# Four heads of values per matmul, and sums of squares from high and low parts, in a transformer block

## The chip, the cores and the metric

The kernel runs on one core of a Trainium2 chip. The metric is the device time of one launch in microseconds (us). Engines are named as in the profile: PE is TensorE (PEld its weight loads), DVE is VectorE, ACT is ScalarE, POOL is GpSimd, and SP is the engine from whose queue all of this kernel's DMAs are issued.

## What is computed

One layer of a hybrid encoder on 1024 tokens with 1024 channels, in float32. Cut to what matters:

```python
u = modulate(rmsnorm(h, g_ff1), sh1, sc1)
h = h + 0.5 * gt1 * swiglu(u, w1_gate, w1_up, w1_down)      # D_FF = 2816
u = modulate(rmsnorm(h, g_mix), sh2, sc2)
proj = u @ w_in
qa, ka, va, xm, o_pre, ga, gb = split(proj)                  # each 1024 wide
ya = diff_attention(rope(qa), rope(ka), va)                  # 8 heads, values 128 wide; rmsnorm per head
yb = mlstm_branch(xm, o_pre)                                 # 4 heads, chunkwise
merged = sigmoid(ga) * (ya @ w_proj_a) + sigmoid(gb) * (yb @ w_proj_b)
h = h + gt2 * (merged @ w_out)
u = modulate(rmsnorm(h, g_ff2), sh3, sc3)
h = h + 0.5 * gt3 * swiglu(u, w2_gate, w2_up, w2_down)
return rmsnorm(h, g_final)
```

Each rmsnorm needs a sum of squares over channels for every token. sh, sc and gt come from the conditioning vector c through w_ada ("ada").

## The kernel before

**Layout.** Channels lie on the 128 partitions, tokens along the free dimension, in two halves of 512. A float32 product is made of three float32r matmuls: an operand is split into a high part (an ACT cast, L126, L137, L143) and a low part (a DVE subtraction, L127, L138, L144), and `mm3` (L132 to L134) adds high x high, high x low and low x high in PSUM. `unit` (L121) loads a weight tile of 128 x 1024 (raw, two buffers in `wraw`) and splits it into a pair wh, wl from the pool `whl`, which has three buffers of each. `t512` hands out one of six shared tiles of 128 x 512.

**Stages, in order.** The first feed-forward block (to some 690 us); the projections in for the mLSTM branch with its convolution and its output gate (`stage_in`, to some 895 us; its first group of three weight units is run half by half in `first_norm` and `group`); `stage_mlstm` (to some 1205 us); `stage_attn` (to some 1800 us); the rest of the gated branch, and `stage_merge` (to some 2027 us); the second feed-forward block with the final norm (`out_tail`, `out_step`).

**Order of the work.** PE runs its instructions in the order in which the program emits them. The other engines and the DMA queue of SP also run in order, but their order is made by a planner (the tile framework) from priorities and its own estimate of durations. In the mLSTM and attention stages `paced` emits the steps of the mixers by due times in a model of PE time, and between them pieces of dense work from a list of jobs: `job_qk` (rotary queries and keys of a head), `job_v` (values), `job_g` (pre-activations of the branch gates), `job_b` (gated mLSTM branch). The string `order` sets their sequence: one job of queries and keys, four of values, then queries, keys and gates. A job yields after six matmuls and says what they cost in the model. In the mLSTM stage the scores of a block are due at t and its values at t + 6, and a pitch is 3.

**Values.** `job_v(hp)` projects the values of two heads: for each of 8 token tiles, 8 channel tiles x 3 matmuls (L899 to L901) with the token tile as weights and 256 columns of w_v moving. Its two weight units stay in place for the whole job. ACT copies the result (L906) into a tile vo of its own, and every second token tile a DMA of 256 KB stores it to `vd` in DRAM. `load_v` in the attention stage reads a head from there.

**Sums of squares.** ACT squares (L208, L605, L1338), DVE adds channel tiles together (L210, L611), and PE sums over partitions with one float32 matmul on a 128 x 128 tile of ones: in `rstd` (L182, at the start of the kernel), `rstd_half` (L215), `out_stat` (L629) and, per head, `norm_items` (L1345, into a PSUM tile oss that shares its one bank with the attention's output po). `rstd_of` (L157) makes the reciprocal root on ACT (L162, L165), in a t512 tile.

Of the kernel before, what the change touches and what calls it, by code (L numbers as in the profile page):

```python
# [20 lines left out]
P = 128  # L21
D = 1024
# [17 lines left out]
class Halves:  # L40
    """two tiles with half of the tokens each"""
# [9 lines left out]
class Net:  # L51
    def __init__(self, ctx, tc, aps, dbg):
# [5 lines left out]
        self.whl = e(tc.tile_pool(name="whl", bufs=3))  # L58
# [7 lines left out]
        nc.vector.memset(self.ones, 1.0)  # L66
        self.zeros = c.tile([P, 64], F32, name="zeros")
# [24 lines left out]
    # conditioning: one column block of w_ada per call  # L92
# [27 lines left out]
    # weights  # L120
# [19 lines left out]
    def split_in(self, hi, lo):  # L140
        """the same of what has been loaded into the place of the low part"""
        raw = lo.bitcast(F32)
        self.nc.scalar.copy(hi, raw)  # L143
        self.nc.vector.tensor_sub(lo, raw, hi.bitcast(F32))  # L144

    def set_lnexp(self, after):
        """have the table set with Ln and Exp loaded behind `after`"""
        t = self.nc.scalar.preload_act_table_set(LNEXP)
        self.after(t, after)
        return t  # L150
# [6 lines left out]
    def rstd_of(self, ps, n, last):  # L157
        """1 / sqrt(ps / n + eps); `last`: the activation before it"""
# [9 lines left out]
    # 1 / rms over channels, on every partition, for some of the tokens  # L168
# [35 lines left out]
    def sum_square(self, n, i, m):  # L204
        """add channel tile m of half n, its i-th, to the running sum of squares"""
# [6 lines left out]

    def rstd_half(self, bank):
        ps = bank()
        self.nc.tensor.matmul(ps, self.ones, self.sq_acc, start=True, stop=True)  # L215
        self.r_half = self.rstd_of(ps, D, self.sq_last)
# [7 lines left out]
    def norm_step(self, i, q, j, bank):  # L224
        """first half's modulation behind the steps of the last products"""
# [8 lines left out]
    def norm_behind(self, i, n, m, bank):  # L234
        """behind the update of channel tile m of half n: statistics, and the first half's modulation"""
# [12 lines left out]
    def group(self, srcs, psp, tag, hook):  # L248
        """several M-tiles of a projection of u at once, channel tile by channel tile"""
# [15 lines left out]
    def ffn(self, wgu, wd, gt, first, plain, hid, after, step, extra=None):  # L265
        """h += gate * (silu(u w_gate) * (u w_up)) w_down; hidden passes through DRAM"""
# [33 lines left out]
    # The hidden layer goes to DRAM as the operands that down() takes: even tiles are its rows b1., odd ones b2.  # L300
# [9 lines left out]
    def store_right(self, hid, f, c2):  # L310
        """what follows from the second token half of tile f"""
# [8 lines left out]
    def store_left(self, hid, f, c1):  # L320
        """what follows from the first token half, behind store_right"""
# [10 lines left out]
    # One level of Strassen's scheme in Winograd's form: 7 products for the 8 of two tiles of w^T u, with  # L332
    # w^T = [a11 a12; a21 a22] (tiles x channel halves) and u = [b11 b12; b21 b22] (channel x token halves)
# [10 lines left out]
    def combine_u(self, x, pool):  # L344
        """t1 = b12 - b11, t2 = b22 - t1, -t4 = b21 - t2 for one channel tile of each half"""
# [20 lines left out]
    def combine_u3(self, x):  # L366
        """t3 = b22 - b12, in the place of b12"""
# [69 lines left out]
    def down(self, wd, gt, hid, psg, tp, after, step):  # L437
        """the same scheme for w_down^T (channel halves x even and odd tiles) and the hidden layer"""
# [63 lines left out]
        # product: its operands, weights to fetch meanwhile, a combination that takes a weight's place  # L502
# [43 lines left out]
    def first_start(self, srcs, psg, gtag, psd, dtag):  # L546
        """the first block's input: statistics, modulation and the first tiles as x and w_ada come in"""
# [42 lines left out]
    def first_norm(self, i, srcs, psg, gtag, psd, dtag):  # L590
        """later blocks' input: the first tiles run on one half while the other is normalised"""
# [8 lines left out]
    def out_tail(self, n, i, m, bank):  # L600
        """final norm behind the last update of h"""
# [23 lines left out]
    def out_stat(self, q, sums, bank):  # L625
        ns = self.spans[q]
        ps = bank()[:, 0:ns.stop - ns.start]
        for i, x in enumerate(sums):
            self.nc.tensor.matmul(ps, self.ones, x, start=i == 0, stop=i == len(sums) - 1)  # L629
# [8 lines left out]
    # one M-tile of a projection of u: PSUM halves  # L638
# [18 lines left out]
    def mix_setup(self):  # L657
# [11 lines left out]
        self.vd = [sc(f"v{h}", [P, 2, 8, P]) for h in range(4)]  # L669
# [4 lines left out]
    def fold_gates(self, hd, psp, tag):  # L674
        """gate weights seen from xc and xm, as [hi | lo] stationary tiles"""
# [32 lines left out]
    def stage_in(self, st):  # L708
        """xm with causal conv and gate pre-activations; sigmoid of the output gate"""
# [178 lines left out]
    # dense work that fills the tensor engine between the steps of the two sequence mixers  # L888
    def job_v(self, hp):
        nc = self.nc  # L890
        w = [self.unit(self.a["wv"][hp, i]) for i in range(2)]
        for tt in range(8):
            ps = self.psdn.tile([P, NW], F32, name=self.nm("vp"), tag="dn")
            tsl = slice(tt * P, tt * P + P)
            o = ps[:, 0:256]
            for k in range(KT):
                wh, wl = w[k // 4]
                ws = slice((k % 4) * 256, (k % 4) * 256 + 256)
                nc.tensor.matmul(o, self.uh[k][:, tsl], wh[:, ws], start=k == 0, stop=False)  # L899
                nc.tensor.matmul(o, self.uh[k][:, tsl], wl[:, ws], start=False, stop=False)  # L900
                nc.tensor.matmul(o, self.ul[k][:, tsl], wh[:, ws], start=False, stop=k == KT - 1)  # L901
                if k % 2:
                    if k == KT - 1:
                        if tt % 2 == 0:
                            vo = self.rope.tile([P, 2, 2, P], F32, name=self.nm("vo"), tag=f"vo{tt // 2 % 2}")
                        nc.scalar.copy(vo[:, :, tt % 2], o.rearrange("p (q c) -> p q c", q=2))  # L906
                        if tt % 2:
                            nc.sync.dma_start(out=self.vd[hp][:, :, tt - 1:tt + 1], in_=vo)
                    yield 6 * 0.11
# [672 lines left out]
```

## Time and profile before

| | |
|---|---|
| median of three timed runs | 2677.02 us (2673.28 to 2679.34) |
| profiled execution, span from the first to the last instruction | 2681.1 us |
| PE busy | 2592.6 us (97%) in 12704 matmuls |
| DVE busy | 1877.3 us (70%) |
| ACT busy | 1288.3 us (48%) |
| mean granted clock of PE | 0.990 |

The page gives no other time of the profiled execution than its span. Matmuls are pipelined: the duration of one in the trace is its latency, and the next one starts before it ends. The granted clock has two levels here, 1.0 (2.4 GHz) and 0.5 (1.2 GHz).

### The profile page before, as it was taken

How to read it: one execution, taken by the hardware profiler on the slowest of the kernel's cores; microseconds unless marked ns; L12 is line 12 of the kernel's file. 1: busy time of each engine (PE TensorE's matmuls, PEld its weight loads, DVE VectorE, ACT ScalarE, POOL GpSimd, SP SyncE). 2: the span in 40 equal slices, each digit the busy share in tenths (PEclk: the TensorE clock that was granted, in tenths of full speed). 3: DMA queues.
4: the chain of work that ended last, by engine and by line, in shares of the span. 5: the costliest groups of instructions: out<-in, count | busy, mean ns of one | idle time of the engine just before them, and what ended most of it. 6: DMA issues, size and time to landing. Idle time of an engine off the chain costs nothing.

```text
span 2681.1 us, 35203 instructions
## 1 busy us (share of the span) xinstructions
PE 2592.6 (97%) x12704; PEld 2155.8 (80%) x12704; DVE 1877.3 (70%) x3352; ACT 1288.3 (48%) x2369; POOL 22.5 (1%) x85
## 2 busy tenths in 40 slices
PE   6999999999899999999999999999999999999998
PEld 4888887778777799997777778777887888888886
DVE  7987878678795456646766766654467776766867
ACT  6333333446435366654666766753345332323444
POOL 0000000000000000000000000000000000000000
PEclk8999999999999999999999999999999999999999
DMA  7434345833674423334333333558342333236533
GB/s 262 162 130 145 118 149 185 274 99 104 215 258 149 140 91 118 111 100 121 111 102 106 99 105 115 159 198 277 131 140 87 110 98 115 99 102 216 161 95 122
DMA packets 174471, 380.47 MB, mean 142 GB/s; under 512 B 18405, under 2 KB 47529, under 8 KB 174297
## 3 DMA queue, kind: packets, MB, share of 16 engines
q1 hardware_dynamic: 174296, 378.24, 43.6%
q8 instruction: 99, 1.62, 0.2%
q14 instruction: 76, 0.61, 0.1%
HBM read 280.27 MB, written 97.90 MB: 141 GB/s over the span
## 4 chain that ended last, share of the span: by engine, by line
PE 84%; DMA 7%; DVE 5%; ACT 3%; issue 1%; SPq 0%; DVEq 0%; ACTq 0%; POOL 0%; POOLq 0%
PE gu L134 10%; PE gu L133 10%; PE gu L132 10%; PE acc L132 5%; PE acc L133 5%; PE acc L134 5%; PE ab L132 2%; PE ab L133 2%; PE ab L134 2%; PE dn L134 2%; PE dn L132 2%; PE dn L133 2%; PE gp L132 2%; PE gp L134 2%; PE gp L133 2%; PE pt L1305 1%
## 5 line engine op out<-in xcount | busy, mean ns | idle before, releaser
L132 PE MATMUL gu<-uh,wh 128*128 128x512 f32 x800 | 314.2, 393 | 10.1 <-ACT uh L201 8.8
L133 PE MATMUL gu<-ul,wh 128*128 128x512 f32 x800 | 313.4, 392 | 1.3 <-DVE ul L202 1.3
L134 PE MATMUL gu<-uh,wl 128*128 128x512 f32 x800 | 313.2, 391 | 0.8 <-DVE wl L127 0.7
L137 ACT CAST wh<-wr 128x512 fp32r<-128x512 f32 x228 | 134.0, 619 | 253.0 <-PE gu L133 194.0
L132 PE MATMUL acc<-uh,wh 128*128 128x512 f32 x616 | 241.9, 393 | 1.3 <-ACT uh L137 1.3
L133 PE MATMUL acc<-ul,wh 128*128 128x512 f32 x616 | 240.3, 390 | 1.3 <-DVE ul L138 1.3
L134 PE MATMUL acc<-uh,wl 128*128 128x512 f32 x616 | 239.8, 389 | 0.0
L126 ACT CAST wh<-wr 128x1024 fp32r<-128x1024 f32 x120 | 125.8, 1049 | 148.0 <-PE wo L133 46.1
L127 DVE TENSOR_TENSOR wl<-wr,wh 128x1024 fp32r<-128x1024 f32 x120 | 146.5, 1221 | 71.8 <-ACT wh L126 70.9
L132 PEld LDWEIGHTS gu<-uh,wh 128*128 128x128 f32 x800 | 151.2, 189 | 44.3 <-ACT uh L201 10.4
L133 PEld LDWEIGHTS gu<-ul,wh 128*128 128x128 f32 x800 | 151.2, 189 | 34.4 <-DVE ul L202 2.3
L134 PEld LDWEIGHTS gu<-uh,wl 128*128 128x128 f32 x800 | 151.1, 189 | 33.4 <-DVE wl L127 2.3
L133 PE MATMUL gu<-ut,wh 128*128 128x512 f32 x456 | 177.5, 389 | 0.0
L132 PE MATMUL gu<-ut,wh 128*128 128x512 f32 x456 | 177.4, 389 | 0.0
L134 PE MATMUL gu<-ut,wl 128*128 128x512 f32 x456 | 177.4, 389 | 0.0
L138 DVE TENSOR_TENSOR wl<-wr,wh 128x512 fp32r<-128x512 f32 x228 | 152.8, 685 | 1.6 <-ACT wh L137 1.6
L137 ACT CAST uh<-hr 128x512 fp32r<-128x512 f32 x154 | 95.4, 619 | 100.2 <-PE acc L134 63.6
L132 PEld LDWEIGHTS acc<-uh,wh 128*128 128x128 f32 x616 | 115.6, 188 | 28.6 <-ACT uh L137 2.5
L133 PEld LDWEIGHTS acc<-ul,wh 128*128 128x128 f32 x616 | 115.6, 188 | 26.3 <-DVE ul L138 2.2
L134 PEld LDWEIGHTS acc<-uh,wl 128*128 128x128 f32 x616 | 115.6, 188 | 24.1
L138 DVE TENSOR_TENSOR ul<-hr,uh 128x512 fp32r<-128x512 f32 x154 | 105.8, 687 | 35.5 <-ACT uh L137 35.0
L1281 ACT ACTIVATE p<-sc,lr 128x256 f32<-128x256 f32 (+7 forms) x128 | 94.8, 741 | 74.0 <-DVE lr L1279 72.1
(335 smaller groups left out, 6561.4 us busy)
## 6 DMA issues: line engine op xcount, KB each, us to landing
ada<-wada SPq DMA_DIRECT2D x72, 512.0 KB
wr<-win SPq DMA_DIRECT2D x48, 512.0 KB
wr<-w1gu SPq DMA_DIRECT2D x44, 512.0 KB
wr<-w2gu SPq DMA_DIRECT2D x44, 512.0 KB
wr<-wab SPq DMA_DIRECT2D x32, 512.0 KB
g<-t SPq DMA_DIRECT2D x32, 256.0 KB
t<-g SPq DMA_DIRECT2D x32, 256.0 KB
wr<-wout SPq DMA_DIRECT2D x16, 512.0 KB
```

Source lines behind the costliest of these rows:

```text
L126: nc.scalar.copy(hi, raw)
L127: nc.vector.tensor_sub(lo, raw, hi.bitcast(F32))
L132: nc.tensor.matmul(ps, w[0], x[0], start=start, stop=False)
L133: nc.tensor.matmul(ps, w[0], x[1], start=False, stop=False)
L134: nc.tensor.matmul(ps, w[1], x[0], start=False, stop=stop)
L137: (eng or self.nc.scalar).copy(hi, src)
L138: self.nc.vector.tensor_sub(lo, src, hi.bitcast(F32))
L1281: nc.scalar.activation(pc[c][:, 0:W], ps[:, 0:W], AF.Exp, bias=lr[:, 2 + c:3 + c], accum_out=lr[:, c:c + 1])
L1305: nc.tensor.transpose(pt[:, kk, i], a[i][:, kb * P:kb * P + P], self.ident)
```

## The change

Values are projected for four heads in a job: four weight units, 512 columns per matmul, two jobs and not four. The result is copied into a shared t512 tile and stored for each token tile. `sum_over` takes the place of the float32 matmul on ones in `rstd_half`, `out_stat` and `norm_items`: it splits its operand into a high and a low part, in two t512 tiles, and runs two float32r matmuls on a float32r tile of ones. `rstd` keeps the float32 matmul. The pool `whl` gets five buffers, and the DMA scratch of the program is set to 1024. Comments go as well.

```diff
-        self.whl = e(tc.tile_pool(name="whl", bufs=3))
+        self.whl = e(tc.tile_pool(name="whl", bufs=5))
...
+        self.onesr = c.tile([P, P], F32R, name="onesr")
+        nc.scalar.copy(self.onesr, self.ones)
...
+    def sum_over(self, ps, x, start=True, stop=True):
+
+        hi, lo = (self.t512()[:, 0:x.shape[1]].bitcast(F32R) for _ in range(2))
+        self.split(x, hi, lo)
+        self.nc.tensor.matmul(ps, self.onesr, hi, start=start, stop=False)
+        self.nc.tensor.matmul(ps, self.onesr, lo, start=False, stop=stop)
+
     def rstd_half(self, bank):
         ps = bank()
-        self.nc.tensor.matmul(ps, self.ones, self.sq_acc, start=True, stop=True)
+        self.sum_over(ps, self.sq_acc)
...
         for i, x in enumerate(sums):
-            self.nc.tensor.matmul(ps, self.ones, x, start=i == 0, stop=i == len(sums) - 1)
+            self.sum_over(ps, x, i == 0, i == len(sums) - 1)
...
-        self.vd = [sc(f"v{h}", [P, 2, 8, P]) for h in range(4)]
+        self.vd = [sc(f"v{h}", [P, 4, 8, P]) for h in range(2)]
...
     def job_v(self, hp):
-        nc = self.nc
-        w = [self.unit(self.a["wv"][hp, i]) for i in range(2)]
+
+        nc = self.nc
+        w = [self.unit(self.a["wv"][hp, i]) for i in range(4)]
         for tt in range(8):
             ps = self.psdn.tile([P, NW], F32, name=self.nm("vp"), tag="dn")
             tsl = slice(tt * P, tt * P + P)
-            o = ps[:, 0:256]
             for k in range(KT):
-                wh, wl = w[k // 4]
-                ws = slice((k % 4) * 256, (k % 4) * 256 + 256)
-                nc.tensor.matmul(o, self.uh[k][:, tsl], wh[:, ws], start=k == 0, stop=False)
-                nc.tensor.matmul(o, self.uh[k][:, tsl], wl[:, ws], start=False, stop=False)
-                nc.tensor.matmul(o, self.ul[k][:, tsl], wh[:, ws], start=False, stop=k == KT - 1)
+                wh, wl = w[k // 2]
+                ws = slice((k % 2) * NW, (k % 2) * NW + NW)
+                nc.tensor.matmul(ps, self.uh[k][:, tsl], wh[:, ws], start=k == 0, stop=False)
+                nc.tensor.matmul(ps, self.uh[k][:, tsl], wl[:, ws], start=False, stop=False)
+                nc.tensor.matmul(ps, self.ul[k][:, tsl], wh[:, ws], start=False, stop=k == KT - 1)
                 if k % 2:
                     if k == KT - 1:
-                        if tt % 2 == 0:
-                            vo = self.rope.tile([P, 2, 2, P], F32, name=self.nm("vo"), tag=f"vo{tt // 2 % 2}")
-                        nc.scalar.copy(vo[:, :, tt % 2], o.rearrange("p (q c) -> p q c", q=2))
-                        if tt % 2:
-                            nc.sync.dma_start(out=self.vd[hp][:, :, tt - 1:tt + 1], in_=vo)
-                    yield 6 * 0.11
+                        vo = self.t512().rearrange("p (q c) -> p q c", q=4)
+                        nc.scalar.copy(vo, ps.rearrange("p (q c) -> p q c", q=4))
+                        nc.sync.dma_start(out=self.vd[hp][:, :, tt], in_=vo)
+                    yield 6 * 0.216
...
-                nc.sync.dma_start(out=v[1].bitcast(F32), in_=self.vd[hd // 2][:, hd % 2])
+                nc.sync.dma_start(out=v[1].bitcast(F32), in_=self.vd[hd // 4][:, hd % 4])
...
-                    nc.tensor.matmul(ps, self.ones, sqs[n], start=True, stop=True)
+                    self.sum_over(ps, sqs[n])
...
-            order = "qvvvvqqqggqggqggqggqgggggggg"
-            src = {"q": [net.job_qk(hd) for hd in range(8)], "v": [net.job_v(hp) for hp in range(4)],
+            order = "qvvqqqggqggqggqggqgggggggg"
+            src = {"q": [net.job_qk(hd) for hd in range(8)], "v": [net.job_v(hp) for hp in range(2)],
...
-    o["wv"] = win[:, 2048:3072].reshape(2, 4, P, 4, 256).transpose(3, 0, 2, 1, 4).reshape(4, 2, P, D)
+    o["wv"] = win[:, 2048:3072].reshape(4, 2, P, 2, NW).transpose(3, 0, 2, 1, 4).reshape(2, 4, P, D)
...
-    nc = _bacc.Bacc("TRN2", target_bir_lowering=False, num_devices=1)
+    nc = _bacc.Bacc("TRN2", target_bir_lowering=False, num_devices=1, dynamic_dma_scratch_size=1024)
```

## Rows read from the trace of the kernel before

**Rows 1.** The head of the page: the span, and PE's busy time.

```profile
span 2681.1 us, 35203 instructions
PE 2592.6 (97%) x12704; PEld 2155.8 (80%) x12704; DVE 1877.3 (70%) x3352; ACT 1288.3 (48%) x2369; POOL 22.5 (1%) x85
```

**Rows 2.** By stretch, us: length, busy PE, PEld, DVE, ACT, POOL, clock, DMA share, GB/s.

```profile
60.00:660.00 600.00, 597.86 (x2634) 486.40 (x2633) 479.56 (x814) 228.75 (x391) 0.00 (x0) 1.00 0.46 150
...
720.00:920.00 200.00, 189.89 (x846) 150.14 (x845) 127.99 (x238) 83.62 (x111) 0.62 (x6) 0.98 0.56 190
920.00:1210.00 290.00, 284.11 (x2260) 274.22 (x2259) 170.37 (x446) 177.12 (x523) 13.94 (x32) 1.00 0.34 108
1210.00:1800.00 590.00, 562.97 (x2835) 464.51 (x2834) 397.85 (x746) 381.92 (x690) 6.49 (x32) 0.99 0.40 120
```

**Rows 3.** PE's groups by line and shape: busy us, mean ns, idle before, releasers.

```profile
L132 PE MATMUL gu<-uh,wh 128*128 128x512 f32 x800 | 314.2, 393 | 10.1 <-ACT uh L201 8.8 <-ACT wh L126 1.3
...
L134 PE MATMUL dn<-uh,wl 128*128 128x512 f32 x256 | 101.1, 395 | 6.5 <-DVE wl L127 6.5
...
L899 PE MATMUL vp<-wh,uh 128*128 128x256 f32 x256 | 73.7, 288 | 0.0
```

**Rows 4.** PE in order of time, value matmuls: start, us, what; twelve from first to last.

```profile
935.08 0.28 PE L899 MATMUL vp<-wh,uh 128*128 128x256 f32 x1
...
936.51 0.28 PE L1135 MATMUL num<-mv,sch 128*128 128x258 f32 x1
```

**Rows 5.** PE in order of time, twelve query matmuls from first to last row.

```profile
927.57 0.39 PE L132 MATMUL qp<-uh,wh 128*128 128x512 f32 x1
...
930.32 0.28 PE L1108 MATMUL pr<-RHL,selr 128*128 128x256 f32 x1
```

**Rows 6.** All engines in order of time, around a sum of squares of the second norm.

```profile
695.66 0.68 DVE L210 TENSOR_TENSOR t<-t,t 128x512 f32<-128x512 f32 x1
...
702.00 1.02 PE L215 MATMUL nps<-t,ones 128*128 128x512 f32 x2
...
703.09 0.40 PE L133 MATMUL dn<-ul,wh 128*128 128x512 f32 x1
```

**Rows 7.** The page's costliest groups: a split of 128 x 512, cast and subtraction.

```profile
L137 ACT CAST uh<-hr 128x512 fp32r<-128x512 f32 x154 | 95.4, 619 | 100.2 <-PE acc L134 63.6
...
L138 DVE TENSOR_TENSOR ul<-hr,uh 128x512 fp32r<-128x512 f32 x154 | 105.8, 687 | 35.5 <-ACT uh L137 35.0
```

**Rows 8.** ACT, DVE and PE in order of time, projections in; idle before in brackets.

```profile
728.03 1.06 ACT L126 CAST wh<-wr 128x1024 fp32r<-128x1024 f32 x1 [8.12 <-PE dn L133]
...
728.35 1.23 DVE L115 SCALAR_TENSOR_TENSOR ada<-ada,crep 128x1024 f32<-128x1024 f32 x1 [2.56 <-DMA ada<-wada]
...
735.41 0.80 PE L134 MATMUL dn<-uh,wl 128*128 128x512 f32 x1 [5.37 <-DVE wl L127]
```

**Rows 9.** Busy time by stretch, as rows 2, behind that wait.

```profile
735.40:740.20 4.80, 4.79 (x11) 3.80 (x12) 4.80 (x5) 0.00 (x0) 0.00 (x0) 0.50 0.96 311
740.20:745.00 4.80, 4.80 (x22) 3.92 (x21) 4.80 (x6) 2.30 (x2) 0.11 (x1) 1.00 0.29 117
```

**Rows 10.** ACT and PE in order of time, a head's norm in attention.

```profile
1378.87 0.69 ACT L162 ACTIVATE t<-oss,epsc 128x512 f32<-128x512 f32 x1 [3.60 <-DMA qk<-t]
...
1379.61 1.12 PE L1345 MATMUL oss<-t,ones 128*128 128x512 f32 x2 [1.81 <-ACT t L162]
```

**Rows 11.** ACT and PE in order of time, the next head's norm.

```profile
1440.65 0.63 ACT L1338 ACTIVATE t<-osb 128x512 f32<-128x512 f32 x1
...
1444.86 1.02 PE L1345 MATMUL oss<-t,ones 128*128 128x512 f32 x2
```

**Rows 12.** All engines in order of time, the last norm of the kernel.

```profile
2668.79 0.63 ACT L605 ACTIVATE t<-h 128x512 f32<-128x512 f32 x1 [1.42 <-DVE h L474]
2669.47 1.13 PE L629 MATMUL acc<-t,ones 128*128 128x512 f32 x2 [0.20 <-ACT t L605]
2670.63 0.69 ACT L162 ACTIVATE t<-acc,epsc 128x512 f32<-128x512 f32 x1 [1.22 <-PE acc L629]
```

## The prediction, made before the change was run

> **What bounds the kernel now.** I read first the head of the page: TensorE (PE) has work in flight for 2592.6 of 2681.1 us [rows 1], so time goes only if PE work or a PE wait goes. The busy time by stage, second, shows where waits are left: in the feed-forward stretch PE is busy 597.9 of 600 us; behind it that falls to 189.9 of 200 (projections in), 284.1 of 290 (mLSTM) and 563.0 of 590 (attention), where VectorE (DVE) and ScalarE (ACT) are busy two thirds of the time [rows 2]. Third, a matmul's listed duration (283 to 288 ns for a value matmul [rows 3]) is its latency, and matmuls overlap; what one costs is the spacing of starts, read from the order in time. Fourth, I looked up what PE waited for where it stood still, to see which of those waits hang on something that the change touches: weight halves (wh, wl) and the six shared 512-wide tiles (t512).
>
> The span is 4.1 us above the median of the three timed runs (2677.0); I sum changes against the span and take them off the median.
>
> **Values, four heads at once.** Removed: 768 matmuls of 256 columns (three lines of 256 [rows 3]); added: 384 of 512. Twelve value matmuls start within 936.51 - 935.08 = 1.43 us, 0.119 us each [rows 4]. Twelve query matmuls of 512 columns in the same stage take 930.32 - 927.57 = 2.75 us, 0.229 us each [rows 5]. 768 x 0.119 = 91.4 us, 384 x 0.229 = 87.9: 3.5 us less on a PE that has no wait in these lines [rows 3]. The time goes only if PE then doesn't wait for the mLSTM steps that run between these pieces: a piece of the filling work is now six matmuls of 512 columns (1.37 us) and not of 256 (0.71). The steps are placed two pitches apart from what they wait for, which is more than one piece, so I take -3.5, with 0 and -5 as ends.
>
> The Trainium skill, "TensorE: Matmul & The Clock Gate", section "Back-to-back issue gap", gives a spacing of N / 2.4 + 2.5 ns for N columns at the full clock, which puts nearly the whole cost on the columns. By it (an estimate) 768 x 109.2 ns = 83.9 us would become 384 x 215.8 ns = 82.9 us, and this part would bring 1.0 us, not 3.5. The rows above, 119 and 229 ns, don't follow it at 256 columns, and I go by them.
>
> The rest of this part costs nothing on the path. The evacuations go from 32 copies of 256 columns to 16 of 512. The stores stay 16 of 256 KB on SP, in runs half as long; behind each stand the loads of the mLSTM heads, as before, and the first reader of a value is the attention stage. The weights stay eight loads of 512 KB. Four weight units must now be held at once; with five pairs one is spare, as with two of three before, and the hand-over from the first job to the second happens once, not three times. There the last two units need a raw buffer and a freed pair in turn; I allow up to 3 us of PE wait in the range and 0 in the sum, since the fourth is needed only three pieces into the job, with mLSTM steps between.
>
> **Sums of squares.** Removed: a float32 matmul on the tile of ones, which the trace records as two. From the start of one to the start of the second matmul behind it are 703.09 - 702.00 = 1.09 us [rows 6]; less one ordinary matmul (0.23) it costs 0.86 us. Added: two matmuls of 512 columns, 0.46 us, so 0.40 less on PE each; and ahead of them an ACT cast (0.62 us) and a DVE subtraction (0.69 us) [rows 7], 1.31 us in series. There are 23: 16 in attention (8 heads, two halves), four between the feed-forward, mixing and merge stages, three for the output. The sums at the start of the kernel stay float32.
> Of the four and the first output sum, the running sum is finished well before its place in PE's order: the one in rows 6 at 695.66 + 0.68 = 696.34, 5.7 us ahead, which holds the split. 5 x 0.40 = -2.0 us.
> The last two stand at the end with nothing beside them. The last Square ends at 2668.79 + 0.63 = 2669.42; the matmul begins at 2669.47 and the logarithm at 2670.63 [rows 12], 1.2 us later. Afterwards a cast, a subtraction and one matmul's latency (0.39 [rows 3]) lie there: 0.62 + 0.69 + 0.39, with hops of 0.05, 1.85 us. +0.6.
> Attention: 16 x 0.40 = -6.4 us of PE. Against that, (i) the split must fit between the Square and the matmul. In the usual case it does: Square ends at 1440.65 + 0.63 = 1441.28, the matmul starts at 1444.86, a gap of 3.6 us [rows 11]; one of the sixteen had no gap, where 1.3 us show. (ii) The sum now takes two of the six t512 tiles, and these are scarce here: once ACT waited 3.60 us for a DMA out of a t512 tile before it could write the reciprocal root, and PE stood 1.81 us at the next sum [rows 10]. Two more of these are 3.6 us. (iii) ACT gets 16 x 0.62 = 9.9 and DVE 16 x 0.69 = 11.0 us more, on 382 and 398 of 590 [rows 2]. Behind them on DVE stand the splits that PE's transposes wait for; that is in (ii)'s allowance. +5 in all, net -1.4. Ends: -6.4 (all hidden) and 16 x (1.31 - 0.40) = +14.6 (all shown).
>
> **Five pairs of split weights, not three.** The diff's first lines raise whl from 3 to 5 and pay with the smaller DMA scratch and the dropped vo tiles. At the start of the projections in, three units are held by the first group until its end. So ACT's cast of the fourth waits 8.12 us until 728.03; behind it DVE, in order, first does ada columns that wait for their loads (2.56 us before one of them); the low half comes so late that PE stands 5.37 us until 735.41 [rows 8]. With five pairs the fourth unit can be split as soon as its load is in, while the first group still runs, and PE has nothing to wait for there: -5.4. The granted clock is 0.50 behind this stall, over 4.8 us with 11 matmuls where the next 4.8 us have 22 [rows 9]; without the stall I expect none of that, -2.4. All other PE waits for wh or wl in the trace are 6.5 - 5.4 = 1.1 (dn) and 1.3 (gu) [rows 3], and fall where a group takes three pairs from the stage before: half of 2.4, -1.2. The feed-forward stretches have nothing to gain, as PE is full there [rows 2]. Together -9.0, ends 0 and -10.5.
>
> **Sum.** -3.5 - 2.0 + 0.6 - 1.4 - 9.0 = -15.3 us: a profile of 2665.8, and 2677.0 - 15.3 = 2661.7 us.
>
> **Rivals.**
> (A) The forecast, 2661.7.
> (B) All splits in attention ride free (-5.0 more) and deeper weights take away some of its own waits, 27 us of PE idle [rows 2], say a fifth (5): -25, 2651.7. For it: casts of weights in attention wait for PE to free a pair, in an in-order queue ahead of the mixers' casts. Against: PE's named waits in that stage are for the attention's own splits.
> (C) The change of depth doesn't do what I say: DVE keeps the ada columns ahead of the low half, and the stall of 5.4 and the slow clock stay. -15.3 + 7.8 = -7.5, 2669.5. For it: that order isn't written in the kernel but comes from a planner. Against: the wait that began it is the freed pair, 8.12 us.
> (D) Half of the attention's splits show: 8 x 1.31 - 6.4 = +4.1, not -1.4, and the hand-over between the value jobs costs 3 us: -15.3 + 5.5 + 3 = -6.8, 2670.2.
> (E) Slower: t512 runs out in attention. A head's turn has two Squares, four halves and two roots, eight tiles for six places, beside the rotary work and the gates, whose tiles wait for DMAs out. If ACT, in order, stands 3.6 us for a place [rows 10] and PE with it, and the clock then drops as in rows 9 (2.4 us), one event costs 6 us. It decides from (15.3 + 5.4) / 6 = 3.5 events on; five give 30 - 15.3 = +15, 2692. For it: rows 10 show the wait. Against: once in 16 so far, and halves are given back as soon as PE has read them.
>
> **How the numbers follow.** A 0.50, B 0.15, C 0.12, D 0.12, E 0.11. About 0.2% (5.4 us) is what a measurement of this kernel can tell from no change: faster means below 2671.6. A and B lie there wholly, C and D by a bit, with half of each over the line when the other terms come out smaller: 0.50 + 0.15 + 0.06 + 0.06 = 0.77. The other halves are within: 0.12. E is slower: 0.11. The range of A alone is about 2654 to 2669; to leave out no more than 2 in 10 it takes in B's centre, C and D and the near edge of E: 2644 to 2679.
>
> **What would show it.** Value matmuls of 512 columns 384 times at 0.229 us, and the mLSTM stretch 3 to 4 us shorter. Sums as pairs of matmuls of 0.23 us; the cast and subtraction between Square and sum in 3 us. No PE wait near 730, no 0.50 clock behind it, and the projections in 8 us shorter. The attention stretch within 5 us of before; a PE wait on the cast of a sum, or ACT on a DMA out of a t512 tile, more than three times there would mean D or E. What would make it wrong: a planner's new order of ACT, DVE and SP that makes a stall elsewhere, above all where the stages meet.

## The result, and the profile after

The changed kernel takes 2703.03 us (median of four runs, 2699.05 to 2706.9), the kernel before 2678.18 (four runs): a ratio of 1.0097, interval 1.0085 to 1.0109, 25 us slower by the medians. I had put 2661.7 first, and a range up to 2679.

Head of the page of the changed kernel, then its busy time by stretch (us: length, busy PE, PEld, DVE, ACT, POOL, clock, DMA share, GB/s), answering [rows 1] and [rows 2]:

```profile
span 2703.0 us, 34689 instructions
...
PE 2591.9 (96%) x12320; PEld 2142.6 (79%) x12320; DVE 1893.9 (70%) x3375; ACT 1301.5 (48%) x2378; POOL 21.8 (1%) x85
```

```profile
60.00:660.00 600.00, 596.42 (x2627) 485.31 (x2627) 480.45 (x815) 228.32 (x392) 0.00 (x0) 1.00 0.46 150
720.00:920.00 200.00, 193.70 (x871) 154.02 (x870) 130.74 (x242) 86.18 (x116) 0.62 (x6) 0.99 0.57 191
920.00:1210.00 290.00, 282.43 (x1872) 254.90 (x1871) 166.13 (x443) 173.65 (x500) 13.29 (x32) 1.00 0.34 104
1210.00:1800.00 590.00, 541.41 (x2714) 447.98 (x2714) 401.27 (x750) 379.58 (x688) 6.51 (x32) 0.97 0.38 113
```

In the projections in, PE is busier by 3.8 us (193.70 against 189.89). In attention it is busy for 21.6 us less of 590 (541.41 against 562.97), with 121 fewer matmuls done, and the mean clock has gone from 0.99 to 0.97, worth 0.02 x 590 = 12 us of full clock. The loss is in attention.

I also measure stages by marks on PE that all kernels share: first matmul of the projections in, first query matmul, first score of attention, last matmul on its output po. Before, these stages take 201.5, 327.5 and 555.2 us; after, 193.7, 330.0 and 583.0. So projections in -7.8, mLSTM +2.5, attention +27.8; what comes behind it is 3.6 us shorter, and the first block 2.9 longer. Together +21.8, the difference of the two spans.

What PE waited for in the changed kernel (us in total, times, longest), the rows for the sums and the one left for the projections in, where no row for a weight half stands any more:

```profile
PE oss L219 <- ACT t L139: 19.3, 9, 6.2
...
PE oss L220 <- DVE t L140: 7.5, 12, 1.7
...
PE dn L134 <- DVE h L483: 2.5, 1, 2.5
```

The sums of attention wait 19.3 us for the cast (L139) and 7.5 for the subtraction (L140): 26.8 us in 21 waits. Before, one wait of 1.8 us [rows 10] and one of 0.6 stood there. The longest, ACT and then PE in order of time (start, duration; idle before in brackets), with the busy time of the stretch behind:

```profile
1446.19 0.63 ACT L1345 ACTIVATE t<-osb 128x512 f32<-128x512 f32 x1
1446.72 0.60 ACT L139 CAST t<-t 128x512 fp32r<-128x512 f32 x1
...
1453.13 1.04 ACT L145 CAST av<-av 128x1024 fp32r<-128x1024 f32 x1 [3.52 <-DMA av<-v]
1454.08 0.62 ACT L167 ACTIVATE t<-t 128x512 f32<-128x512 f32 x1
1454.62 0.57 ACT L944 COPY t<-qp 128x512 f32<-128x512 f32 x1
1455.08 1.04 ACT L128 CAST wh<-wr 128x1024 fp32r<-128x1024 f32 x1
...
1457.41 0.61 ACT L139 CAST t<-t 128x512 fp32r<-128x512 f32 x1
```

```profile
1447.38 0.50 PE L219 MATMUL oss<-t,onesr 128*128 128x512 f32 x1 [1.28 <-ACT t L139]
...
1458.07 0.79 PE L219 MATMUL oss<-t,onesr 128*128 128x512 f32 x1 [6.20 <-ACT t L139]
1459.76 0.80 PE L220 MATMUL oss<-t,onesr 128*128 128x512 f32 x1 [0.90 <-DVE t L140]
```

```profile
1454.40:1464.40 10.00, 5.43 (x12) 3.97 (x13) 8.14 (x13) 4.33 (x8) 0.00 (x0) 0.50 0.32 96
1464.40:1474.40 10.00, 10.00 (x53) 8.47 (x53) 5.40 (x12) 6.00 (x12) 0.20 (x1) 1.00 0.25 93
```

The Square of the second half (L1345) ends at 1446.82. Its cast starts at 1457.41, 10.6 us later, behind a load of values on which ACT stands 3.52 us, a root, a copy, the cast of a weight and an exponential. Note the first cast shown, of the first half: it too stands only behind the second half's Square, 3.9 us after its own. Over the sixteen sums of attention the cast starts 0.8 to 36 us behind the end of its Square, 4.6 at the median; PE waits where the matmul is due earlier than that.

Before, the matmul read the Square itself, so ACT had nothing more to do for it [rows 11]. ACT stood as long for a load of values there too, but the sum's matmul, at 1444.86, did not depend on what stood behind. ACT in the trace of before:

```profile
1447.82 1.05 ACT L143 CAST av<-av 128x1024 fp32r<-128x1024 f32 x1 [3.71 <-DMA av<-v]
```

The first of the two stretches of 10 us above begins 3.7 us before the wait ends; PE's granted clock is 0.50 in it, and it has 12 matmuls where the next has 53. In all, attention has eight stretches at 0.50 in the trace of after, 38 us together, and five of them (27 us) begin in or right behind waits of a sum; before, it had three, 14 us.

The values do what they were to do: 384 matmuls of 512 columns, six of them here within one piece, 0.23 us apart, as [rows 5].

```profile
931.90 0.40 PE L908 MATMUL vp<-wh,uh 128*128 128x512 f32 x1
...
933.05 0.39 PE L910 MATMUL vp<-wh,ul 128*128 128x512 f32 x1
934.81 0.39 PE L908 MATMUL vp<-wh,uh 128*128 128x512 f32 x1
```

### The profile page after: what moved, and what is told of

Its sections match the earlier page's. It is cut to its first block, busy times and chain, and to the rows that moved or that the text cites. A ratio compares the mean times of both kernels' runs of the same rounds, so it can differ in the third digit from the quotient of the medians.

```text
span 2703.0 us, 34689 instructions
## 1 busy us (share of the span) xinstructions
PE 2591.9 (96%) x12320; PEld 2142.6 (79%) x12320; DVE 1893.9 (70%) x3375; ACT 1301.5 (48%) x2378; POOL 21.8 (1%) x85
## 4 chain that ended last, share of the span: by engine, by line
PE 56%; DMA 5%; DVE 5%; ACT 3%; issue 1%; SPq 0%; DVEq 0%; ACTq 0%
PE gu L136 5%; PE gu L134 5%; PE gu L135 5%; PE acc L134 3%; PE acc L136 3%; PE acc L135 3%; PE ab L134 2%; PE ab L135 2%; PE ab L136 2%; PE gp L134 2%; PE gp L135 2%; PE gp L136 2%; PE wo L135 1%; PE wo L134 1%; PE wo L136 1%
## 5 line engine op out<-in xcount | busy, mean ns | idle before, releaser
L139 ACT CAST wh<-wr 128x512 fp32r<-128x512 f32 x228 | 133.8, 620 | 220.9 <-PE gu L135 194.9
L139 ACT CAST uh<-hr 128x512 fp32r<-128x512 f32 x154 | 95.1, 619 | 133.4 <-PE acc L136 54.8
L140 DVE TENSOR_TENSOR wl<-wr,wh 128x512 fp32r<-128x512 f32 x228 | 152.6, 686 | 2.5 <-ACT wh L139 2.4
L140 DVE TENSOR_TENSOR ul<-hr,uh 128x512 fp32r<-128x512 f32 x154 | 105.6, 687 | 36.8 <-ACT uh L139 36.7
```

Of the source, the lines that this page charges most:

```text
L139: (eng or self.nc.scalar).copy(hi, src)
L140: self.nc.vector.tensor_sub(lo, src, hi.bitcast(F32))
```

## The experiments

Times are medians, each against the runs of the kernel before on the same chip (2677.8 to 2680.3 in the batches below). The ratio weighs all runs, and by it a difference comes out up to some 2 us other than by the medians; both are given where that matters. Single executions of one kernel differ by up to some 10 us either way, so stage lengths of single traces are read with that in mind.

**The sums of attention taken back.** The changed kernel with L1352 as before:

```diff
-                    self.sum_over(ps, sqs[n])
+                    nc.tensor.matmul(ps, self.ones, sqs[n], start=True, stop=True)
```

> The changed kernel with one part undone: the sums of the attention's norms go back to the float32 matmul. Theory Q (the cast and the subtraction of these sums stand in ACT's and DVE's queues and PE waits for them, 19.3 + 7.5 us of waits plus slow clock): the attention stretch falls back by 25 to 30 us, the whole to 2673 to 2680 us. Rival T (the stretch is longer for another reason: the values now take t512 tiles, or five pairs of weights reorder the queues): no more than 10 us come back, 2693 us or more.

Measured: 2678.15, ratio 0.9991 (0.9978 to 1.0004), 25 us faster than the changed kernel. Attention takes 555.8 us. The whole loss goes with these 16 sums.

**The sums of attention alone.** The kernel before, three pairs and narrow values, with the 16 sums split as in the change, in t512 tiles.

```diff
-                    nc.tensor.matmul(ps, self.ones, sqs[n], start=True, stop=True)
+                    hi, lo = (self.t512().bitcast(F32R) for _ in range(2))
+                    self.split(sqs[n], hi, lo)
+                    nc.tensor.matmul(ps, self.onesr, hi, start=True, stop=False)
+                    nc.tensor.matmul(ps, self.onesr, lo, start=False, stop=True)
```

> The kernel before with the attention's sums alone as two passes in t512 tiles, three pairs of weights, values as before. Theory: the splits wait for places in t512 and in ACT's queue whatever the rest does, so 15 to 30 us more than before: 2692 to 2707 us. Rival: it takes the deeper weights or the values' use of t512 to make it slow: within 8 us of before.

Measured: 2705.92, ratio 1.0111 (1.0097 to 1.0126), 28 us slower than before. Attention takes 584.4 us. What PE waited for, as above:

```profile
PE oss L1349 <- ACT t L139: 26.0, 11, 6.7
...
PE oss L1350 <- DVE t L140: 7.3, 11, 3.0
```

So neither the wide values nor the five pairs are needed for the loss. In the longest of these waits the shared tiles show directly: the cast of the sum at 1379.76 has 4.71 us of idle ACT before it, ended by a DMA out of a t512 tile (`qk<-t`), and PE waits 6.69 us for that cast.

**Tiles of their own.** The changed kernel; the halves of a sum of attention go into two own tiles and not into t512, at the same place in the program.

```diff
-                    self.sum_over(ps, sqs[n])
+                    hi, lo = (a1.tile([P, NW], F32R, name=self.nm("so"), tag=f"so{c}", bufs=1) for c in "hl")
+                    self.split(sqs[n], hi, lo)
+                    nc.tensor.matmul(ps, self.onesr, hi, start=True, stop=False)
+                    nc.tensor.matmul(ps, self.onesr, lo, start=False, stop=True)
```

> The changed kernel with a high and a low tile of their own for the attention's sums in place of two t512 tiles. If places in t512 are what delays the cast (my prediction's rival E), 15 us or more come back: 2688 us or less. If it is the place of the cast in ACT's queue, behind loads of values, copies and weight casts, little comes back: 2695 to 2705 us.

Measured: 2680.89, ratio 1.0007 (0.9994 to 1.0019): 22 of the 25 us are back. Attention takes 559.1 us, and the sums wait 7.2 us, 2.5 of them for a root (L164) and not for a split. The casts now start 0.6 us behind their Squares at the median, and 4.7 at most.

```profile
PE oss L1355 <- DVE so L140: 2.9, 5, 1.1
PE oss L1354 <- ACT t L164: 2.5, 1, 2.5
...
PE oss L1354 <- ACT so L139: 1.8, 2, 0.9
```

**The split earlier.** The changed kernel, still with t512 tiles, but the program emits the split behind the Square and not with the matmul.

```diff
-                        sqs.append(sq)
+                        hl = [self.t512().bitcast(F32R) for _ in range(2)]
+                        self.split(sq, *hl)
+                        sqs.append(hl)
```

> The changed kernel with the split of the attention's sums written out right behind each Square, a piece of work earlier, and still in t512 tiles (four are held until the matmuls, not two). Theory Q: PE then finds both halves ready at most sums, 20 us or more come back, 2683 us or less, and PE's waits on these sums fall from 27 to under 8 us. If places in t512 are the cause: more tiles held for longer, as slow or slower, 2700 us or more.

Measured: 2681.04, ratio 1.0007 (0.9997 to 1.0018): the same 22 us. Attention takes 563.1, and the sums wait 7.9 us, 3.3 of them for a split:

```profile
PE oss L1354 <- ACT t L139: 1.8, 2, 0.9
...
PE oss L1355 <- DVE t L140: 1.5, 3, 0.7
```

The casts start 0.15 us behind their Squares at the median. Either of the two cures alone does it, so the loss needs both: a late place in the program and shared tiles. How the two together lead the planner to put the casts so late is not shown; that it waits for shared tiles to come free is how I read it.

**Both cures.** The changed kernel with the early split into four own tiles.

```diff
-                        sqs.append(sq)
+                        hl = [a1.tile([P, NW], F32R, name=self.nm("so"), tag=f"so{c}{n}") for c in "hl"]
+                        self.split(sq, *hl)
+                        sqs.append(hl)
```

> The change with the attention's sums split early, right behind the Square, into four tiles of their own, and values in pieces of six matmuls as in the change. It differs from the version with pieces of three (2672.2) in the pieces alone, and from the change with float32 sums in attention (2678.2) in the sums alone. If the sums with free places and an early split bring what PE saves (16 x 0.40 us) less small waits: 2672 to 2675, attention 552 to 557 us. If the smaller pieces were what brought the gain: 2676 to 2679. If the early split into own tiles brings no more than an early split in shared tiles or own tiles late: about 2681.

Measured: 2676.27, ratio 0.9991 (0.9981 to 1.0001). The sums wait 4.1 us, and attention takes 553.9. With float32 sums the same kernel has the same ratio, 0.9991 (by the medians the two passes are 1.9 us faster): here they take the loss away and bring no gain that can be told. What is left:

```profile
PE oss L1354 <- ACT so L139: 2.1, 3, 0.9
...
PE oss L1355 <- DVE so L140: 2.0, 4, 0.7
```

**The same sums on the kernel before,** with three pairs, narrow values and a DMA scratch of 512 (to fit):

> The kernel before with the attention's sums split early into four tiles of their own, a scratch of 512, and three pairs as before. PE saves 16 x 0.40 = 6.4 us, less waits of 1 to 3 us: 3 to 6 us faster than before if the parts add up. If sums and pairs help each other (the cast of weights waits less in ACT's queue with four pairs, and with it the casts of the sums): no more than 3 us faster, or as before.

Measured: 2673.65, ratio 0.9986 (0.9974 to 0.9999), 6.1 us faster than before by the medians, 3.8 by the ratio. Attention takes 549.3 us, the shortest of all. With their places free, the two passes are worth 4 to 6 us, near what PE saves by them (6.4).

**More pairs, with one tile vo.** The kernel before with five pairs, a scratch of 1024, and one of the two tiles vo given up to make room.

```diff
-        self.whl = e(tc.tile_pool(name="whl", bufs=3))
+        self.whl = e(tc.tile_pool(name="whl", bufs=5))
...
-                            vo = self.rope.tile([P, 2, 2, P], F32, name=self.nm("vo"), tag=f"vo{tt // 2 % 2}")
+                            vo = self.rope.tile([P, 2, 2, P], F32, name=self.nm("vo"), tag="vo0")
```

> The kernel before with five pairs of split weights alone (and the small DMA scratch; to find the room, one vo tile and not two). The prediction's step: the PE wait of 5.4 us in the projections in goes, and the slow clock behind it, 8 us less: 2667 to 2671 us. Rival: deeper weights reorder the queues in attention too and lengthen it by 5 us or more: 2675 us or more.

Measured: 2684.6, ratio 1.0017 (1.0003 to 1.0031). It says nothing on the pairs, because the single vo made a stall of its own. A row of PE's waits:

```profile
PE qp L132 <- ACT vo L906: 11.6, 1, 11.6
```

**Five pairs alone.** Both tiles vo kept, a scratch of 512.

> The kernel before with five pairs of split weights alone, both vo tiles kept (a still smaller DMA scratch makes the room). In e4_depth_alone PE stood 11.6 us at the end of the mLSTM stage for a copy that waited for the one vo tile; if that is what spoilt it, this is 2669 to 2675 us, with the projections in 4 to 8 us shorter. If the depth itself costs what it saves: 2677 us or more.

Measured: 2673.18, ratio 0.9989 (0.9978 to 1.0), 4.6 us faster than before (2.9 by the ratio). The wait of [rows 8] is gone.

**Four pairs alone,** with the same scratch, and **the scratch alone:**

> The kernel before with four pairs of split weights and a DMA scratch of 512, nothing else. It differs from the version with four pairs and early sums (16.9 us faster than before) in the sums alone, and from the version with five pairs (4.6 faster) in one pair. If four pairs are worth what five are: 4 to 6 us faster than before, and the sums brought some 12. If the fifth pair costs (new waits behind weights split too early, as for h in the convolution): 8 to 11 us faster, and the sums brought 6 to 8.

> The kernel before with the DMA scratch of 512 alone. I have put all of the gain of the versions with more pairs down to the pairs; if the scratch is without effect, this is within 2 us of before. If it is the scratch that brings part of it, it is 3 us or more faster.

Measured: four pairs 2668.43, ratio 0.9966 (0.9953 to 0.9979), 11.3 us faster than before (9.1 by the ratio). The scratch alone 2680.32, ratio 1.001 (1.0 to 1.002): nothing gained by it. So the gain is the pairs', and a fifth takes part of it back: 4.6 against 11.3, with intervals that only touch. The place that I can name is the first matmul of the projections in, behind the first block; PE in order of time, five pairs and then four:

```profile
692.33 0.50 PE L132 MATMUL dn<-uh,wh 128*128 128x512 f32 x1 [2.50 <-DVE h L474]
```

```profile
690.18 0.50 PE L132 MATMUL dn<-uh,wh 128*128 128x512 f32 x1 [0.84 <-DVE h L474]
```

With five, DVE's last updates of h come later, in another order of weight splits and ada columns ahead of them. That is 1.7 us of the 6.7; the rest I could not place. The wait belongs to the fifth pair and not to one execution: it is 2.1 to 2.8 us in all ten traces with five pairs, and 0.8 to 0.9 in the seven with three or four.

**The kernel before, once more.** One profiled execution.

> The kernel before once more, one profiled execution. What it tells: whether the wait of 5.4 us for a weight half at the start of the projections in, with the slow clock behind it, belongs to every execution. Theory S (it does): the profile shows PE waiting about 5.4 us for wl near 730 us, and the stage between the first matmul of the projections in and the first query matmul takes about 201 us again. Then five pairs bring 8 us there in every run, and what is missing of it in the times (4.6 us measured) is given back later. Theory V (it varies): the wait is under 2 us, the stage takes some 195 us, and the 4.6 us are the mean of runs with and without it.

The wait of [rows 8] is 1.70 us here, not 5.37, and the stage takes 195.6 us, not 201.5. PE in order of time:

```profile
731.08 0.50 PE L134 MATMUL dn<-uh,wl 128*128 128x512 f32 x1 [1.70 <-DVE wl L127]
```

In the three other traces with three pairs (the scratch alone, the early sums, the sums alone) the longest of these waits is 2.7, 2.2 and 1.5 us. The execution that I read had the worst of the five: the wait is always there, its length varies.

**The wide values without any new sum.** The changed kernel with all three places of `sum_over` back in float32; against five pairs alone it differs in the values (and the scratch, 1024).

> The change without any of its new sums of squares: 512-column values for four heads, five pairs of split weights, scratch of 1024. Five pairs alone were 4.6 us faster than before (2673.2). Theory W (wider pieces delay the mLSTM steps, which eats the 3.5 us that PE saves): 2675 to 2679, 1 to 5 us slower than five pairs alone, the mLSTM stage about 2 us longer than before's 327.5. Theory P (the values bring what their spacing says): 2669 to 2671, the mLSTM stage at 324 to 325.

Measured: 2680.08, ratio 1.0 (0.9991 to 1.0008). Five pairs alone gained 4.6 us and this loses 0.8, so by the medians the values cost 5.4 us, by the ratios 2.9, each with some 4 us of uncertainty. The gain of 3.5 that I had counted is not there; that the values cost time is not clear of the noise. The mLSTM stage takes 330.1 us (five pairs alone 328.0; 327.5 and 327.6 in the two executions of before). The six kernels with these values in pieces of six take 329.6 to 330.9, 330.1 on the mean; the eight traces with the old values and both tiles vo 326.9 to 330.9, 328.2 on the mean. PE should have saved 3.5 there.
PE's waits of the mLSTM's first matmuls, five pairs alone and then with the wide values:

```profile
PE vps L1084 <- DVE mv L138: 3.4, 4, 2.7
...
PE qkp L132 <- ACT wqk L137: 1.4, 3, 0.5
```

```profile
PE vps L1091 <- DVE mv L140: 4.7, 5, 3.0
...
PE qkp L134 <- ACT wqk L139: 1.8, 3, 0.9
```

Attention, too, takes 2.4 us longer than with five pairs alone (555.5 against 553.1), with 5.6 us of waits of scores for a cast of keys where there were 0.5. What moved that cast I did not find out.

**Values in smaller pieces.** `job_v` yields after three matmuls and not six, first with float32 sums in attention, then with the early sums in own tiles:

```diff
-                if k % 2:
-                    if k == KT - 1:
...
-                    yield 6 * 0.216
+                if k == KT - 1:
...
+                yield 3 * 0.216
```

> e1_attn_f32 with the value job yielding after three matmuls of 512 columns (0.69 us) and not six (1.37). If the coarse pieces are why the mLSTM steps wait longer (26.4 us over the pure spacing, 20.7 before) and eat the 3 us that the values save, the stretch from the first query to the first score falls by 3 to 5 us against e1_attn_f32 (329.6 to 325 or 326). If the waits come from somewhere else (t512 tiles, depth), it stays within 1.5 us.

> The changed kernel with the attention's sums split right behind the Squares and into tiles of their own, and value pieces of three matmuls. If places and order were the whole cost of the sums, the attention stretch (first score to last value product) falls below before's 555.2 us by up to 6.6, to 549 to 553, and the whole to 2666 to 2673 us, faster than both. If waiting for a split is dear wherever it is put: 558 us and more there, 2676 us or more.

Measured: 2676.69, ratio 0.9998 (0.9989 to 1.0006), and 2672.19, ratio 0.9981 (0.9968 to 0.9995). The mLSTM stage falls to 327.0 and 325.9 us, 2.6 and 4.0 less than the same kernels with pieces of six, and below all six traces with such pieces: the coarse pieces did hold up the steps between them. In the whole time it is worth 0.3 us in the first case (0.8 below before, now 1.1) and 2.5 in the second (3.0, now 5.6), neither clear of its interval; attention grows by 2.9 and 2.6 us.

**The parts that gain, together.** Four pairs and the early sums in own tiles, on the narrow values; scratch 512.

> The kernel before with four pairs of split weights (the fifth does not fit beside the two tiles vo), a DMA scratch of 512, and the attention's sums as two passes, split early into four tiles of their own. Values stay at two heads and 256 columns. Theory W (the wide values cost more than PE saves by them, five pairs and early sums with free places are what gains): 2667 to 2671, so 1 to 5 us faster than the version with wide values in pieces of three (2672.2), mLSTM stage at 327 to 328, attention 548 to 553. Rival: early sums gain only where the value job has given its two tiles vo free and attention's casts move with it, or the fifth pair is what the gain of 4.6 us hangs on: 2674 to 2679.

Measured: 2663.33, ratio 0.9933 (0.9918 to 0.9949), 16.9 us faster than before and faster than both kernels. The parts measured alone give 11.3 + 6.1 = 17.4 (by the ratios 9.1 + 3.8 = 12.9, against 18.0): within what can be told, they add up or better. A sum of attention in it, all engines' rows for one half (Square, cast, subtraction, two passes):

```profile
1432.25 0.63 ACT L1340 ACTIVATE t<-osb 128x512 f32<-128x512 f32 x1
...
1433.62 0.61 ACT L139 CAST so<-t 128x512 fp32r<-128x512 f32 x1
```

```profile
1434.26 0.69 DVE L140 TENSOR_TENSOR so<-t,so 128x512 fp32r<-128x512 f32 x1 [0.87 <-ACT so L139]
```

```profile
1436.03 0.39 PE L1349 MATMUL oss<-so,onesr 128*128 128x512 f32 x1
1436.25 0.39 PE L1350 MATMUL oss<-so,onesr 128*128 128x512 f32 x1
```

The cast starts 0.7 us behind the end of its Square, only a root between them, and the split ends at 1434.95, 1.1 us ahead of its matmul, which waits for nothing.

## Why the prediction was wrong, step by step

The measured times part the 25 us by steps, each against before: five pairs -4.6; the wide values on top (-4.6 to +0.8) +5.4; the inner sums and the tail on top (+0.8 to -0.8) -1.6; the sums of attention on top (-0.8 to +24.9) +25.7. Each step is uncertain by some 4 us either way. By the ratios the steps are -2.9, +2.9, -2.4 and +28.4. Only the last is clear of the noise beyond doubt.

**Attention's sums: the step that failed,** -1.4 forecast, +25.7 measured (+28 alone). The 6.4 us of PE are real. What failed is (i) and (ii) of that part. In (i) I asked whether the split fits between Square and matmul, took the gap of 3.6 us [rows 11] for the usual case, and found 1.31 us of work for it. The gap is usual: fifteen of the sixteen are 2.5 us or longer in the trace of before. But I took for granted that ACT would do the cast at once. The diff emits the split with the matmul, behind what else is due by then, and into shared tiles, and ACT's order put the cast 4.6 us behind its Square at the median, 10.6 at the longest wait. With tiles of their own it is 0.6 from the same place in the program. Nor was ACT free in the gap of [rows 11]: five other instructions of its queue start in it, and behind them comes the stand of 3.71 us for a load of values shown above. In (ii) I had seen that the six places were scarce [rows 10] and priced it at 5 us. The upper end of +14.6 was wrong in kind: it took the split's own 1.31 us as the most that one sum could show, while a wait in order behind other work has no such bound. Closing it by rows: waits at the sums 26.8 - 2.4 = 24.4, slow clock 12, less 6.4 saved, gives 30; the stage grew by 27.8 (some of the slow clock lies in the waits themselves, where it costs nothing). The share of the clock is what I had taken from [rows 9], only it came after many waits and not one.

The Trainium skill, "TensorE: Matmul & The Clock Gate", section "HAM oscillation — how this bites in real kernels", tells of a kernel in which each wait for data sends TensorE back to half clock, and counts half of the slow time as lost. This case's traces agree on the half: 11 matmuls in 4.8 us at 0.50 and 22 in the next 4.8 us at 1.00 [rows 9]. They do not show it for each wait: five slow stretches came with the 21 waits of the sums.

**Rival E** (0.11) had the cause, places in t512 and an event price with the clock in it, and the sign. Two things were off in it. It wanted ACT to stand for a DMA out of a t512 tile, while in the trace of after ACT does other work ahead of the late casts: the scarcity shows as order, not as idle time. (In the sums alone one cast did stand so, for 4.71 us.) And its price of 6 us per event with 3.5 events to decide was met by 21 waits, most of them smaller. Its 2692 stops 11 us short. My mark for it, a wait on a sum's cast more than three times, was met with nine.

**The five pairs.** -9.0 forecast, -4.6 measured at five, -11.3 at four. The mechanism was right: no wait near 730 and no slow clock there. That the stage went down by 7.8 us, just 5.4 + 2.4, is luck of two executions: over the five traces with three pairs it takes 195.6 to 201.5 us, 197.5 on the mean, and over the twelve with more pairs 192.3 to 199.6, 194.5 on the mean. The size came from one execution that had 5.37 us where four others have 1.5 to 2.7, so the stall and the clock behind it are worth less on the mean than the 7.8 I wrote, and the gain of four pairs lies partly elsewhere. Of the other waits for weight halves, those at dn (1.1 us) are gone and those at gu (1.3) stand as before; 0.7 us more of them at gu I had left out. That a fifth pair could cost, I had not considered.

**The values.** Spacing right (0.23 us), 3.5 us saved on PE, but +5.4 measured (+2.9 by the ratios), outside my ends of 0 and -5, though by the ratios 0 lies within the noise. The hand-over between the jobs cost nothing: no wait stands at a value matmul. I argued that two pitches between the steps are more than one piece, so that nothing would wait. The smaller pieces speak against it: with three matmuls to a piece the stage gave back 2.6 to 4.0 us. The rest is in attention, and open.

The spacing that I quoted from the Trainium skill, "TensorE: Matmul & The Clock Gate", section "Back-to-back issue gap", is there that of an isolated matmul, and the page says that it is off for a stream of weight loads and matmuls; the 1.0 us worked out from it decided nothing in the sum.

**Inner sums and tail.** -2.0 + 0.6 = -1.4 forecast, -1.6 measured, the same within what can be told. The two passes between the stages stand 0.22 us apart, with no wait:

```profile
704.34 0.39 PE L136 MATMUL dn<-uh,wl 128*128 128x512 f32 x1
704.57 0.39 PE L219 MATMUL nps<-t,onesr 128*128 128x512 f32 x1
704.79 0.39 PE L220 MATMUL nps<-t,onesr 128*128 128x512 f32 x1
705.02 0.39 PE L134 MATMUL dn<-uh,wh 128*128 128x512 f32 x1
```

That is 0.45 us where 0.86 was [rows 6]. The tail cost more than I said. ACT, PE and ACT again at the end, answering [rows 12]:

```profile
2689.85 0.63 ACT L614 ACTIVATE t<-h 128x512 f32<-128x512 f32 x1 [1.42 <-DVE h L483]
2690.39 1.12 ACT L139 CAST t<-t 128x512 fp32r<-128x512 f32 x2
...
2691.04 0.49 PE L219 MATMUL acc<-t,onesr 128*128 128x512 f32 x1 [2.05 <-ACT t L139]
...
2692.91 0.69 ACT L164 ACTIVATE t<-acc,epsc 128x512 f32<-128x512 f32 x1 [1.40 <-PE acc L220]
```

From the end of the last Square (2690.48) to the logarithm are 2.4 us, before 1.2: +1.2, not +0.6, because two casts stand there, the earlier sum's with the last one's. It was emitted with its matmul, so the same fault in small.

**The odds.** I gave 0.77 to faster. The trace of before showed the scarce places and the in-order queues, and the change put two more tiles and two more queue entries into each of 16 sums in just that stage. I counted the busy time of these and not their order, and so gave the slower side 0.11.

## What to carry to other kernels

When an edit puts a new step on another engine between a producer and PE, ask where that step will stand in the engine's queue, not whether it fits the gap: emit it right behind its producer or give it a tile of its own (either brought 22 of the 25 us back here), or a saving of 0.4 us becomes a wait of up to 6. A stall read in one execution is one sample; before it is put into a sum, look for it in a second one. And coarser pieces of filling work can cost the steps that run between them as much as PE gains by the wider matmuls.

## What was not expected of the hardware

Two things. Behind the wait of 6.20 us the granted clock stayed at 0.50 for 6.4 us after PE had work again, with a second wait of 0.90 us in them; behind the 5.37 us of [rows 8] it was back to 1.00 after 4.8 us [rows 9]. And the wait of [rows 8] lasted from 1.5 to 5.4 us in five executions, with the same code in that stage: one profile gives its place but not its size.
